# Low parts of weights by an accumulating DMA, and a fourth unit of weights ahead

## The chip, the cores and the metric

One core of a Trainium2 chip runs the whole program. The metric is the device time of one execution in microseconds (us). A change of less than 0.2% of it, about 4 us here, can't be told from no change.

## The reference, cut to what matters

Two layers of an encoder over 1024 tokens and 1024 channels, in float32. `w_in` projects the normalised input `h` into the inputs of four mixers (Fourier, convolution, dilated window attention, pooling) and four gate paths; the gated mixer outputs are projected, weighted and projected once more:

```python
h = rms_norm(x, norm_g)
z = h @ w_in                                   # 1024 x 4352
...
for n, y in enumerate(branch_outs):
    y_n = (y * gate_paths[:, :, n]) @ w_branch[n]          # 256 x 1024
    mg = jax.nn.sigmoid(h @ w_gate[n] + b_gate[n])         # 1024 x 1024
    merged = mg * y_n if merged is None else merged + mg * y_n
return x + merged @ w_out                                  # 1024 x 1024
```

## The kernel before

Every operand of TensorE (PE) is a pair: `hi`, the value rounded to fp32r, and `lo`, the rest of it. A product is three matmuls: hi by hi, hi by lo, and lo by hi (`passes`, L129). The pairs are made by `split` (L105, L106): ScalarE (ACT) copies the float32 source into `hi`, and VectorE (DVE) writes `lo` as the source minus `hi`.

Weights come in units of 128 x 1024 (512 KB), by `load_unit` (L108): SyncE (SP) issues the load into one of two raw buffers `wr` (L116), and `split` makes two tiles `w` of it. The tiles stand in a ring of 6 (tag "w"), so three units are held at a time; `weight_form` takes tiles of the same ring for the gates (`wf`). A raw buffer is free again when its last reader, DVE's subtraction, is done. `high_priority(offset=AHEAD)` lets a scheduler place these instructions some 100 instructions early in the queues; each engine then runs its own queue strictly in order.

A layer goes through these stages (times of layer 0):

- up to 500 us: the input units (`in_unit`: one unit by 2 halves of the tokens, 48 matmuls of 512 columns). Between the matmuls, `tick` lets in pieces of the attention (products `s`, exponentials `p`, transposes `pt`, products `pv`, evacuations `o`), of the convolution's 31 taps (`cv`, on DVE) and of the Fourier mixer. DVE also makes `pl`, the low part of the transposed probabilities.
- 500 to 590 us: `branch`, 8 units by 48 matmuls, whose results `y` go to DRAM on SP's queue.
- 590 to 909 us: `gates`. Results `y` are read back on GpSimd's queue (POOL, L993).
- 909 to 1000 us: `out_proj`. The merged parts `mt` are loaded by SP and split into `m` (by `merged`), beside 8 units of `w_out` for each half of the tokens, 24 matmuls a unit. The last layer cuts its second half into quarters and keeps some units.

Four of POOL's instructions are small memsets of `up` (L621, L622) for the next layer. The first input units of a layer, and those of `begin`, use `load_unit` as well.

Of the kernel before, what the change touches and what calls it, by code (L numbers as in the profile page):

```python
# [10 lines left out]
F32R = mybir.dt.float32r  # L11
AF = mybir.ActivationFunctionType
ALU = mybir.AluOpType

P = 128
S = 1024
H = 512
KC = 8
# [3 lines left out]
NEG = -8e30  # L22
SLOTW = 1040
SLOTP = 1088
AHEAD = 100
LAG = 4
LAGT = 2
# [6 lines left out]
KEPT = (None, None, None, "H", "H", "H", "H", "M")  # L34
# [12 lines left out]
class Net:  # L47
# [37 lines left out]
    def slot(self, name, dt=F32, w=S, tag="A"):  # L85
        shape, bufs = {"H": (S, NH), "M": (S, NM), "A": (SLOTP, NA)}[tag]
        return self.sp.tile([P, shape], dt, tag=tag, name=name, bufs=bufs)[:, :w]
# [17 lines left out]
        self.nc.scalar.activation(out=hi, in_=src, func=AF.Copy)  # L105
        self.nc.vector.tensor_tensor(out=lo, in0=src, in1=hi.bitcast(F32), op=ALU.subtract)  # L106

    def load_unit(self, src, kc=KC, n=P, tag=None, ahead=AHEAD):  # L108

        raw = self.raw()  # L110
        flat = raw.rearrange("p k n -> p (k n)")[:, :kc * n].rearrange("p (k n) -> p k n", n=n)
        place = (lambda: self.slot("w", F32R, tag=tag)) if tag else (
            lambda: self.wp.tile([P, KC, P], F32R, tag="w", name="w", bufs=6).rearrange("p k n -> p (k n)"))
        out = [place()[:, :kc * n].rearrange("p (k n) -> p k n", n=n) for _ in range(2)]
        with self.tc.high_priority(offset=ahead):
            self.nc.sync.dma_start(out=flat, in_=src)  # L116
            self.split(*out, flat)
        return out

    def raw(self):  # L120
# [137 lines left out]
    def begin(self, units):  # L258
# [59 lines left out]
        for u, evac in later[3:]:  # L318
            self.half_unit(w_in(u, ahead=AHEAD), 1, evac)

# [3 lines left out]
        evac(hf, ps)  # L324

    def in_unit(self, l, u, evac):
        w = self.load_unit(self.a["w_in"][l, u])
        for hf in range(2):
            self.half_unit(w, hf, evac)

# [503 lines left out]
    def conv_slot(self, dt=F32):  # L834
        return self.sp.tile([P, SLOTP], dt, tag="C", name="cv", bufs=1)[:, :2 * H + 2 * PAD]

# [92 lines left out]

    def branch(self, l, n, g):  # L930
        for u in range(2):
            wh, wl = self.load_unit(self.a["w_branch"][l, n, u])
            for dd in range(4):
                for hf in range(2):
                    ps = self.aux("py") if (dd + hf) % 2 else self.mm("py")
                    self.gemm(ps, [v[:, 2 * dd:2 * dd + 2] for v in (wh, wl)], g, hf)
                    y = self.t2("y")
                    self.nc.scalar.activation(out=y, in_=ps, func=AF.Copy)  # L938
                    self.nc.sync.dma_start(out=self.y[l][n, 4 * u + dd, :, hf * H:hf * H + H], in_=y)
# [27 lines left out]
            yield  # L967

    def weight_form(self, src):
        f = self.wp.tile([P, KC, P], F32R, tag="w", name="wf", bufs=6)  # L970
        self.split(f[:, 0:4], f[:, 4:8], src)
        return f[:, 0:4], f[:, 4:8]

# [5 lines left out]
    def weight_forms(self, l):  # L979
# [4 lines left out]
        for dp in range(4):  # L984
            for n in ORDER:
                raw = self.raw(), self.spare(flip)
                flip = 1 - flip
                ys = [self.slot(f"y{d}", tag="A") for d in range(2)]
                with self.tc.high_priority(offset=AHEAD):
                    for r, d in zip(raw, range(2)):  # L990
# [96 lines left out]
    def out_proj(self, l, tail):  # L1087
        nc = self.nc
        last = l == DEPTH - 1
        xin = self.a["xT"] if l == 0 else self.x1  # L1090
        if not last:
            self.h = self.new_h()
        ms = [[], []]
        self.start("m", self.merged(l, 0, "A", tail, ms[0]))
        self.finish("m")
        self.start("m", self.merged(l, 1, "H", tail, ms[1]))
        kept = {}
        Q = H // 2
        for o, n in ((0, H), (H, Q), (H + Q, Q)) if last else ((0, H), (H, H)):
            hf, off = o // H, o % H  # L1100
            sl = slice(o, o + n)
            xs = []
            self.finish("m") if hf else None
            m = [{hf: [x[:, off:off + n] for x in xk[hf]]} for xk in ms[hf]]
            acc = self.t2("acc")[:, :n]
            for d in range(KC):
                w = kept.get(d) if n < H else None
                if last and n == H and d >= 5:
                    kept[d - 2] = self.load_unit(self.a["w_out"][l, d - 2], tag="H")
                if w is None:  # L1110
                    w = self.load_unit(self.a["w_out"][l, d], tag=KEPT[d] if n < H else None)
                if n < H:
                    kept[d] = w
                ps = self.mm("op")[:, :n]
                self.gemm(ps, w, m, hf)
                if d % (S // n) == 0:
                    group = self.slot(f"xn{d}", tag="M").rearrange("p (d t) -> p d t", t=n)
                x = group[:, d % (S // n)]
                with self.tc.high_priority(offset=AHEAD):
                    nc.sync.dma_start(out=x, in_=xin[d, :, sl])  # L1120
                nc.vector.tensor_tensor(out=x, in0=ps, in1=x, op=ALU.add)
                if not last:
                    nc.sync.dma_start(out=self.x1[d, :, sl], in_=x)
                self.sq_acc(acc, x, d == 0)
                xs.append(x)
            if last:
                def emit(k, t, sl=sl):
                    nc.sync.dma_start(out=self.a["out"][k, :, sl], in_=t)
                self.start("norm", self.norm(acc, xs, lambda k: self.fg[:, k:k + 1], emit, f"f{o}"))
            else:  # L1130
                self.start("norm", self.norm(acc, xs, lambda k: self.p(l + 1, C_G + k), self.h_emit(self.h, hf), f"n{l}_{hf}"))
        if last:
            self.finish("norm")
# [138 lines left out]
```

## Time and profile before

| | us |
|---|---|
| median of 3 runs (lowest to highest) | 1987.56 (1986.22 to 1989.28) |
| the profiled execution: its own time | 1990.16 |
| its span, first to last instruction | 1988.4 |
| PE busy (share of the span) | 1948.0 (98%) |
| DVE busy | 1485.0 (75%) |
| ACT busy | 999.9 (50%) |
| POOL busy | 41.1 (2%) |

The profiled execution took 1.8 us around its span, and 2.6 us more than the median. Busy times are sums over the span. Matmuls overlap and their ends are modelled, so PE's 98% still holds short waits, and what counts is which wait of PE ends last in a stage. The granted TensorE clock was 0.998 of full speed over the span, that is, its upper level of 2.4 GHz nearly throughout.

### The profile page before, as it was taken

The page shows a single profiled execution, that of the slowest core. Times are in us where ns is not written, and L with a number is a line of the kernel's source. Part 1 is how long each engine was busy: PE and PEld are TensorE (multiplying, and loading weights), DVE is VectorE, ACT ScalarE, POOL GpSimd, SP SyncE. Part 2 cuts the span into 40 slices and gives each one's busy share as a digit, 9 for nine tenths or more (in the row PEclk, how much of TensorE's full clock was granted, in tenths as well). Part 3 has the DMA queues.
Part 4 walks back from the last instruction along what each step waited for, and adds up shares of the span by engine and source line. Part 5 has one row for each costly group of instructions (what it writes and reads, how often), then busy time and mean ns, then how long its engine had stood idle before and what let it go on. Part 6 is the DMA issues. An engine that isn't in the chain of part 4 may idle for free.

```text
span 1988.4 us, 26782 instructions
## 1 busy us (share of the span) xinstructions
PE 1948.0 (98%) x9484; PEld 1624.7 (82%) x9484; DVE 1485.0 (75%) x2740; ACT 999.9 (50%) x1917; POOL 41.1 (2%) x90
## 2 busy tenths in 40 slices
PE   8999999999999999999999999999999999999997
PEld 6788887888888888887888888888888888888887
DVE  7598878886577777776655888888564877787764
ACT  6336655568574344444431456656775644443441
POOL 0000000000000000000000000000000000000000
PEclk9999999999999999999999999999999999999999
DMA  6243344423774433427421534433248823424443
GB/s 237 78 149 117 102 131 120 128 67 107 247 276 167 156 106 108 157 76 259 163 81 45 159 117 126 133 106 106 87 139 295 287 85 127 136 99 146 170 148 107
DMA packets 129446, 281.08 MB, mean 141 GB/s; under 512 B 32928, under 2 KB 37920, under 8 KB 129312
## 3 DMA queue, kind: packets, MB, share of 16 engines
q1 hardware_dynamic: 118368, 239.52, 37.0%
q0 software_dynamic: 10944, 39.85, 6.0%
q8 instruction: 75, 1.23, 0.3%
q14 instruction: 59, 0.48, 0.1%
HBM read 186.84 MB, written 67.30 MB: 128 GB/s over the span
## 4 chain that ended last, share of the span: by engine, by line
PE 81%; DVE 9%; ACT 4%; DMA 4%; issue 2%; SPq 0%; DVEq 0%; ACTq 0%
PE z L129 24%; PE ga L129 13%; PE g L129 9%; PE gb L129 8%; PE op L129 8%; PE py L129 8%; PE z L256 3%; DVE cv L849 2%; PE pv L129 2%; PE s L466 2%; PE pt L492 1%; DVE w L106 1%; ACT w L105 1%; ACT o L523 1%; DMA mt<-m 1%
## 5 line engine op out<-in xcount | busy, mean ns | idle before, releaser
L129 PE MATMUL z<-h,w 128*128 128x512 f32 x3000 | 741.4, 396 | 2.5 <-DVE gp L610 1.4
L129 PEld LDWEIGHTS z<-h,w 128*128 128x128 f32 x3000 | 546.8, 188 | 109.1 <-DVE gp L610 1.8
L106 DVE TENSOR_TENSOR w<-wr,w 128x1024 fp32r<-128x1024 f32 (+1 forms) x135 | 158.7, 1178 | 106.8 <-ACT w L105 90.9
L105 ACT ACTIVATE w<-wr 128x1024 fp32r<-128x1024 f32 (+1 forms) x135 | 137.9, 1023 | 172.7 <-PE z L129 80.3
L129 PE MATMUL g<-h,wf 128*128 128x512 f32 x768 | 184.5, 389 | 0.0
L129 PE MATMUL ga<-t,wf 128*128 128x512 f32 x768 | 184.5, 389 | 0.0
L129 PE MATMUL gb<-t,wf 128*128 128x512 f32 x768 | 184.5, 389 | 0.0
L129 PE MATMUL op<-m,w 128*128 128x512 f32 (+1 forms) x960 | 179.8, 348 | 2.8 <-DVE m L106 2.7
L849 DVE SCALAR_TENSOR_TENSOR cv<-cv,params 128x512 f32<-128x512 f32 x240 | 179.1, 746 | 2.3
L129 PE MATMUL py<-g,w 128*128 128x512 f32 x768 | 178.4, 391 | 0.8 <-DVE gp L610 0.5
L129 PEld LDWEIGHTS op<-m,w 128*128 128x128 f32 x960 | 153.9, 189 | 27.1 <-DVE m L106 4.4
L129 PEld LDWEIGHTS py<-g,w 128*128 128x128 f32 x768 | 143.1, 188 | 31.7 <-ACT y L938 1.3
L129 PEld LDWEIGHTS ga<-t,wf 128*128 128x128 f32 x768 | 144.2, 188 | 29.9
L129 PEld LDWEIGHTS gb<-t,wf 128*128 128x128 f32 x768 | 144.2, 188 | 29.9
L129 PEld LDWEIGHTS g<-h,wf 128*128 128x128 f32 x768 | 144.2, 188 | 29.9
L105 ACT ACTIVATE wf<-wr 128x512 fp32r<-128x512 f32 x144 | 91.0, 632 | 117.6 <-issue 46.3
L106 DVE TENSOR_TENSOR wf<-wr,wf 128x512 fp32r<-128x512 f32 x144 | 98.8, 686 | 19.4 <-ACT wf L105 18.1
L480 ACT ACTIVATE p<-p,nm 128x256 f32<-128x256 f32 (+2 forms) x192 | 87.9, 459 | 42.7 <-DVE nm L477 42.4
L105 ACT ACTIVATE wf<-s 128x512 fp32r<-128x512 f32 x64 | 40.5, 632 | 105.2 <-PE gb L129 62.6
L129 PE MATMUL ga<-h,wf 128*128 128x512 f32 x384 | 92.2, 389 | 0.0
L523 ACT ACTIVATE o<-pv 64x128 f32<-64x128 f32 x192 | 67.5, 351 | 48.1 <-PE pv L129 46.2
L129 PEld LDWEIGHTS ga<-h,wf 128*128 128x128 f32 x384 | 72.1, 188 | 15.0
(244 smaller groups left out, 2683.0 us busy)
## 6 DMA issues: line engine op xcount, KB each, us to landing
wr<-in_w_in_dram SPq DMA_DIRECT2D x75, 512.0 KB, 3.8
y<-y SPq DMA_DIRECT2D x128, 256.0 KB, 4.1
y<-y POOLq DMA_DIRECT2D x64, 512.0 KB, 4.8
wr<-in_w_gate_dram SPq DMA_DIRECT2D x48, 512.0 KB, 4.4
wr<-in_w_out_dram SPq DMA_DIRECT2D x32, 512.0 KB, 3.6
rot<-rt SPq DMA_DIRECT2D x192, 64.0 KB, 2.0
cv<-in_w_gate_dram SPq DMA_DIRECT2D x16, 512.0 KB, 4.9
wr<-in_w_branch_dram SPq DMA_DIRECT2D x16, 512.0 KB, 4.7
```

The source lines that it names most:

```text
L105: self.nc.scalar.activation(out=hi, in_=src, func=AF.Copy)
L106: self.nc.vector.tensor_tensor(out=lo, in0=src, in1=hi.bitcast(F32), op=ALU.subtract)
L129: self.nc.tensor.matmul(ps, w, x, start=(first and i + u == 0), stop=(i == n - 1 and u == 2), skip_group_check=open_)
L256: self.nc.tensor.matmul(ps, a[:, k], b, start=(k + j == 0), stop=(k == KC - 1 and j == 2))
L466: mm(s[i][h], q[h + j][:, qs], k[h][:, a:a + n], start=(j == 0), stop=(j == 2))
L480: nc.scalar.activation(out=ph, in_=ph, func=AF.Exp, bias=nm[:, h:h + 1], accum_out=st[:, t, 2 + h:3 + h])
L492: nc.tensor.transpose(pt[:rows[ci], cs], p[:, off:off + rows[ci]], self.ident)
L523: nc.scalar.activation(out=dst, in_=src, func=AF.Copy)
L849: self.tc.keep_in_program_order(nc.vector.scalar_tensor_tensor(out=y, in0=u[:, j:j + H], scalar=tap(j), in1=y, op0=ALU.mult, op1=ALU.add))
```

## The change

`load_unit` gets a second way (`late=True`). ACT writes minus the high part into the `lo` tile, then the high part into the `hi` tile, both from the raw buffer; a DMA on POOL's queue then reads the same weights from DRAM a second time and adds them onto the `lo` tile. DVE takes no part. It is used for the input units that go through `in_unit`, for all units of `branch`, and for the units of `out_proj` with d > 0 (those that are kept ahead for the last quarters stay as they were): 96 units in all, 26 and 29 of `w_in`, 16 of `w_branch`, 14 and 11 of `w_out`. The ring of `w` tiles grows from 6 to 8, so four units are held; the space for descriptors of GpSimd's DMAs falls from 8192 to 2048 bytes.

```diff
+NWT = 8
...
-    def load_unit(self, src, kc=KC, n=P, tag=None, ahead=AHEAD):
+    def load_unit(self, src, kc=KC, n=P, tag=None, ahead=AHEAD, late=False):
...
-            lambda: self.wp.tile([P, KC, P], F32R, tag="w", name="w", bufs=6).rearrange("p k n -> p (k n)"))
+            lambda: self.wp.tile([P, KC, P], F32R, tag="w", name="w", bufs=NWT).rearrange("p k n -> p (k n)"))
...
             self.nc.sync.dma_start(out=flat, in_=src)
-            self.split(*out, flat)
+            if late:
+                self.nc.scalar.activation(out=out[1], in_=flat, func=AF.Copy, scale=-1.0)
+                self.nc.scalar.activation(out=out[0], in_=flat, func=AF.Copy)
+                self.nc.gpsimd.dma_start(out=out[1], in_=src, accum_op=ALU.add)
+            else:
+                self.split(*out, flat)
...
-        w = self.load_unit(self.a["w_in"][l, u])
+        w = self.load_unit(self.a["w_in"][l, u], late=True)
...
-            wh, wl = self.load_unit(self.a["w_branch"][l, n, u])
+            wh, wl = self.load_unit(self.a["w_branch"][l, n, u], late=True)
...
-        f = self.wp.tile([P, KC, P], F32R, tag="w", name="wf", bufs=6)
+        f = self.wp.tile([P, KC, P], F32R, tag="w", name="wf", bufs=NWT)
...
-                    w = self.load_unit(self.a["w_out"][l, d], tag=KEPT[d] if n < H else None)
+                    w = self.load_unit(self.a["w_out"][l, d], tag=KEPT[d] if n < H else None, late=d > 0)
...
-    nc = _bacc.Bacc("TRN2", target_bir_lowering=False, num_devices=1, dynamic_dma_scratch_size=8192)
+    nc = _bacc.Bacc("TRN2", target_bir_lowering=False, num_devices=1, dynamic_dma_scratch_size=2048)
```

The new lines move the numbers below them by one to six: L105 and L106 become L106 and L107, and the two new ACT copies are L119 (minus the high part) and L120 (the high part).

The order in which instructions stand shows what moves. First DVE in the attention of layer 0, at the piece of one head pair in which `qa` and `qb` are rotated and a `pl` is made. Before:

```order
L106 TENSOR_TENSOR w<-wr,w 128x1024
L382 TENSOR_TENSOR qa<-rot,qa 64x4x128
L382 TENSOR_TENSOR qb<-rot,qb 64x4x128
L849 SCALAR_TENSOR_TENSOR cv<-cv,params 128x512
L375 TENSOR_TENSOR rc<-rt,cos 128x512
L849 SCALAR_TENSOR_TENSOR cv<-cv,params 128x512
L106 TENSOR_TENSOR pl<-pt,ph 128x256
```

Now:

```order
L573 TENSOR_TENSOR xm<-xm,nat_2938 128x16
L388 TENSOR_TENSOR qa<-rot,qa 64x4x128
L388 TENSOR_TENSOR qb<-rot,qb 64x4x128
L855 SCALAR_TENSOR_TENSOR cv<-cv,params 128x512
L107 TENSOR_TENSOR pl<-pt,ph 128x256
```

The subtraction `w` ahead of these is gone, and `rc` and a tap `cv` now stand elsewhere. Next ACT at the end of layer 0's gates, where the first units of `out_proj` are split (`c`, `p` are gates, `m` the merged parts). Before:

```order
L1047 ACTIVATE p_8196<-g 128x512
L105 ACTIVATE wf<-wr_8072 128x512
L105 ACTIVATE w<-wr 128x1024
L1036 ACTIVATE c_8227<-g,params 128x512
L105 ACTIVATE w<-wr 128x1024
L105 ACTIVATE m_8293<-mt 128x512
```

Now:

```order
L106 ACTIVATE w<-wr 128x1024
L1042 ACTIVATE c_8103<-c_8103,params 128x512
L1053 ACTIVATE p_8230<-g 128x512
L119 ACTIVATE w<-wr 128x1024
L1042 ACTIVATE c_8261<-g,params 128x512
L120 ACTIVATE w<-wr 128x1024
L119 ACTIVATE w<-wr 128x1024
L120 ACTIVATE w<-wr 128x1024
L1042 ACTIVATE c_8277<-c_8277,params 128x512
L106 ACTIVATE m_8327<-mt 128x512
```

The first unit (d = 0, not late) stands earlier by the two tiles that the ring gained; the second and third (d = 1, 2) follow as pairs of copies ahead of the first `m`. Last SP at the same place. Before:

```order
L116 DMA wr<-in_w_out_dram 128x1024 x2
L1120 DMA xn_8381<-in_xT_dram 128x512 x2
L1120 DMA xn_8470<-in_xT_dram 128x512 x2
L1120 DMA xn_8545<-in_xT_dram 128x512 x2
L1120 DMA xn_8620<-in_xT_dram 128x512 x2
L116 DMA wr<-in_w_out_dram 128x1024
L1080 DMA mt<-m_78 128x512 x6
L116 DMA wr<-in_w_out_dram 128x1024
```

Now:

```order
L117 DMA wr<-in_w_out_dram 128x1024 x2
L1126 DMA xn_8415<-in_xT_dram 128x512 x2
L117 DMA wr<-in_w_out_dram 128x1024
L1126 DMA xn_8506<-in_xT_dram 128x512 x2
L1126 DMA xn_8583<-in_xT_dram 128x512 x2
L1126 DMA xn_8660<-in_xT_dram 128x512
L117 DMA wr<-in_w_out_dram 128x1024
L1086 DMA mt<-m_78 128x512 x9
L117 DMA wr<-in_w_out_dram 128x1024
```

The load just ahead of the `mt` loads was the third of `w_out` (d = 2) and is now the fourth (d = 3).

## Rows read from the trace of the kernel before

**Rows 1.** The page: busy time by engine, and the chain that ended last by engine.

```profile
PE 1948.0 (98%) x9484; PEld 1624.7 (82%) x9484; DVE 1485.0 (75%) x2740; ACT 999.9 (50%) x1917; POOL 41.1 (2%) x90
...
PE 81%; DVE 9%; ACT 4%; DMA 4%; issue 2%; SPq 0%; DVEq 0%; ACTq 0%
```

**Rows 2.** The page's groups (part 5): the weight split, xcount | busy us, mean ns | idle before.

```profile
L106 DVE TENSOR_TENSOR w<-wr,w 128x1024 fp32r<-128x1024 f32 (+1 forms) x135 | 158.7, 1178 | 106.8 <-ACT w L105 90.9
L105 ACT ACTIVATE w<-wr 128x1024 fp32r<-128x1024 f32 (+1 forms) x135 | 137.9, 1023 | 172.7 <-PE z L129 80.3
```

**Rows 3.** What PE waited for, whole span: us in total, times, longest.

```profile
PE pv L129 <- DVE pl L106: 2.6, 3, 0.9
...
PE fb L594 <- ACT o L523: 2.2, 2, 1.1
...
PE pt L492 <- DVE nm L477: 1.3, 1, 1.3
...
PE z L129 <- ACT rt L371: 1.1, 1, 1.1
PE pt L492 <- ACT o L523: 0.8, 2, 0.5
```

**Rows 4.** Timeline of PE at three waits: start us, us, what [idle before <- releaser].

```profile
283.87 0.30 PE L466 MATMUL s<-kb,qb 128*128 128x128 f32 x1 [0.62 <-DVE pl L106]
...
303.51 0.39 PE L129 MATMUL pv<-pl,vfh 128*128 128x256 f32 x1 [0.87 <-DVE pl L106]
...
515.17 1.17 PE L129 MATMUL py<-g,w 128*128 128x512 f32 x4 [0.53 <-DVE gp L610]
```

**Rows 5.** Timeline of DVE ahead of the second of these waits.

```profile
298.46 1.22 DVE L106 TENSOR_TENSOR w<-wr,w 128x1024 fp32r<-128x1024 f32 x1
...
303.04 0.42 DVE L106 TENSOR_TENSOR pl<-pt,ph 128x256 fp32r<-128x256 f32 x1
```

**Rows 6.** Chain that ended last, 895 to 925 us: start us, us, what.

```profile
895.55 2.73 PE g L129 x12
...
898.36 1.24 DVE w L106
...
899.62 0.33 SPq L116
...
900.52 7.14 DMA mt<-m
...
913.38 1.14 DVE w L106
...
915.16 0.61 DVE m L106
...
915.82 9.21 PE op L129 x39
```

**Rows 7.** Windows: busy us (instructions) of PE, PEld, DVE, ACT, POOL; PEclk; DMA share, GB/s.

```profile
100.00:500.00 400.00, 389.41 (x2062) 326.61 (x2061) 327.42 (x728) 233.93 (x544) 0.00 (x0) 1.00 0.39 114
...
480.00:600.00 120.00, 117.49 (x532) 95.38 (x531) 79.73 (x141) 75.81 (x132) 1.19 (x2) 1.00 0.74 257
900.00:910.00 10.00, 10.00 (x46) 8.29 (x45) 5.61 (x9) 3.92 (x6) 0.00 (x0) 1.00 1.02 360
940.00:950.00 10.00, 10.00 (x45) 8.27 (x45) 4.38 (x6) 2.28 (x4) 0.00 (x0) 1.00 0.47 160
```

**Rows 8.** The page: DMA issues, median us from issue to landing.

```profile
y<-y POOLq DMA_DIRECT2D x64, 512.0 KB, 4.8
...
m<-y POOLq DMA_DIRECT2D x12, 512.0 KB, 6.4
```

**Rows 9.** Chain that ended last, whole span: one stretch of back-to-back matmuls.

```profile
1013.74 78.91 PE z L129 x348
```

**Rows 10.** Timeline of ACT, a gate of the last product.

```profile
898.31 0.69 ACT L1036 ACTIVATE c<-g,params 128x512 f32<-128x512 f32 x1 [1.61 <-PE g L129]
```

**Rows 11.** Timeline of POOL: the second pair of memsets.

```profile
933.16 0.10 POOL L621 MEMSET up<- 128x8 f32 x1 [17.80 <-DVE m L106]
```

## The prediction

> **What bounds the kernel now.** I read the page's busy times and chain first: PE is busy 1948.0 us of 1988.4 and is 81% of the chain that ended last, DVE 9%, ACT 4% [rows 1]. So the most that any change of the other engines can return is PE's own waits, 40.4 us by these rows, part of them the start and the end. Next the groups of the weight split: a subtraction of DVE costs 1.18 us, a copy of ACT 1.02 us, 135 of each [rows 2]. Then the view of waits, for PE alone. The reader is to see that no row there says that PE waited for a weight tile `w`: PE waits for DVE's `pl` and `nm`, and for ACT's `o` and `rt`, one to three times each [rows 3]. So the change can't gain by bringing weights sooner, only by what leaving DVE and loading ACT does to those other waits. The timelines tell which wait had a weight subtraction in front of it. Before three waits of PE, of 0.62, 0.87 and 0.53 us [rows 4], DVE had worked without a pause from a subtraction to the releaser; for the second the rows show 1.22 us of `w` at 298.46 and the late `pl` at 303.04 [rows 5]. Last the chain at the start of layer 0's `out_proj`: a product of the gates ends, DVE subtracts the first unit, that frees a raw buffer for SP's next `w_out` load, behind that load stand the `mt` loads, 7.14 us to land, then the splits of `m` with another weight subtraction of 1.14 us among them, then PE [rows 6]. Layer 1 has the same chain.
>
> **The change, step by step.** DVE loses 96 subtractions, ACT gains 96 copies, POOL gains 96 DMAs. In layer 0's attention (100 to 500 us) about 26 of them fall: 26 x 1.18 = 31 us off DVE's 327 (9%), 26 x 1.02 = 27 us onto ACT's 234 (11%) [rows 2, 7].
>
> *Subtractions directly ahead of a wait.* The three waits above are each shorter than the 1.18 us taken from the run of work before them, so all go: 0.62 + 0.87 + 0.53 = **-2.0 us**. What may be late next there is ACT, whose copy precedes the `lo` part; the bound is nothing gained.
>
> *DVE's other waits in the attention.* `pl` keeps 2.6 - 0.9 = 1.7 us and `nm` 1.3 us [rows 3], with no weight subtraction in the run before. DVE has 9% less to do, but its taps `cv` fill the gaps. Between 0 and -3.0 us I take a third: **-1.0 us**.
>
> *ACT's waits.* PE waited 2.2 + 1.1 + 0.8 = 4.1 us for ACT's `o` and `rt` [rows 3]. One copy of 1.02 us more per unit stands in the same queue, and whatever is behind a copy that waits for a free tile waits too. Between 0 and twice as much (+4.1) I take a third: **+1.4 us**.
>
> *What the adding DMA costs.* The trace holds none. The nearest rows: a plain load of 512 KB on POOL's queue lands 4.8 us after its issue, a store 6.4 us [rows 8]. For the engines' time: 257 GB/s at a share of 0.74 [rows 7] makes 347 GB/s at a full share, so 512 KB copied once is 1.5 us of all 16 engines. The adding DMA reads the source, reads the tile and writes it: one pass, 1.5 us, from below, three passes, 4.5 us, from above. I take two, 3.0 us, since source and tile are both read. In `branch` a unit lasts 48 matmuls of 78.91 / 348 = 0.227 us [rows 9], 10.9 us: 0.74 + 3.0 / 10.9 = 1.02 of the engines. In `out_proj` a unit lasts 24 of these, 5.44 us: 0.47 [rows 7] + 3.0 / 5.44 = 1.02. The attention, at 0.39, has room. A share of 1.02 was reached in the trace, at 360 GB/s [rows 7]. So it just fits, and costs **0**.
>
> That an adding DMA has two reads is also what the Trainium skill says (Collectives: The Full Stack, "Why ReduceScatter is half of AllGather"): the addition itself is free, the second source read halves the rate. By it the price would be 3.0 us and the sum unchanged; no run here shows it yet.
>
> *Arrival of the low part.* With four units held, a tile is freed three units before its use: 3 x 5.44 = 16.3 us in `out_proj`, 32.7 us elsewhere. After that come a copy (1.02), then the adding DMA (6.4 if it lands like the slower row): 8.9 us to spare at the tightest place. **0**; a landing of 15 us would use it up.
>
> *The start of `out_proj`.* The subtraction at 913.38 leaves the chain: -1.14. But the order on SP now puts the fourth `w_out` load ahead of the `mt` loads. It needs the raw buffer of d = 1, and that is free only after both its copies. The first, into the `lo` tile, waits for the same product that ends at 898.28 (895.55 + 2.73) [rows 6]; then come 1.02, a gate of 0.69 [rows 10] and 1.02: 901.0, against 899.6 before. So the `mt` loads start 1.4 us later. Together +0.3 a layer, less a little for an addition of the gates that the order puts ahead of the first `m`: **0** for both layers, bounds -2.3 and +2.8.
>
> *POOL's queue.* Two pairs of memsets stand between layer 0's `w_out` additions, and wait for DVE. The second ran at 933.2 [rows 11]; the addition behind it is d = 6. PE reaches d = 6 five units after d = 0 ends: 39 matmuls from 915.82 [rows 6] less 35 of them give 916.7, plus 5 x 5.44 = 943.9. That is 10.7 us later, 4 us more than a landing. **0**.
>
> Sum: -2.0 - 1.0 + 1.4 = -1.6. The profiled execution took 1990.16 us (span 1988.4 and 1.8 around it): 1988.6. It lies 2.6 above the median, so the median becomes **1986.0 us**. About 0.2%, 4 us, can be told from no change.
>
> **Rivals.**
> *DVE's relief works fully.* The three waits, the other 3.0 us and the 2.3 us at both starts of `out_proj` go, and ACT, busy for about 60% of the attention, hides its copies: -7.3, 1980.3. For it: DVE was over 80% busy in the attention against ACT's 58% [rows 7]. Against it: ACT feeds most of these chains.
>
> *The `mt` loads are held up.* From 900 to 910 us the engines were already at 1.02 [rows 7]. The additions of d = 1 and d = 2 now fall there, 3.0 us each beside six `mt` loads of 256 KB. If one of them delays the first `mt` by its whole 3.0 us, PE waits 3.0 a layer: +6.0, 1992.0. It decides once the first `mt` takes about a microsecond more than 7.14. Against it: `m` beyond the first is limited by DVE, not by DMA.
>
> A page of the Trainium skill (DMA: Bandwidth & Descriptors, "Issuing engines are not separate DMA queues") would put POOL's DMAs on the same 16 engines as SP's, interleaved; that speaks for this rival, and no row of before shows the two together here.
>
> *The adding DMA takes three passes.* Then `out_proj` needs 0.47 + 4.5 / 5.44 = 1.30. Over layer 0's 16 units, 87 us, that is 26 us of backlog less 8.9 to spare: +17; over the 38 us of the last layer's seven late units before the quarters 11 - 9 = +2; `branch` at 1.15 builds 13 us, which its 25 to spare hide. 1986.0 + 19 = 2005. It decides above two passes.
>
> **How the numbers follow.** The forecast, within 4 us of before, gets 0.42; full relief 0.30; late `mt` loads 0.15; three passes 0.10; 0.03 for something else. The likeliest case's own range is 1983.6 to 1991.5. Both signs are possible, so the range runs from below full relief (less 2.3 for a start of `out_proj` that loses more than its subtraction), 1978, to between late `mt` loads and three passes, 1998; outside lie most of the three passes and some of the relief, less than 2 in 10. Faster by over 0.2%: 0.32; within: 0.42; slower: 0.26.
>
> **What would show it.** Of DVE: 96 groups of `w` less, and `pl` no longer among PE's longest waits. Of ACT: `o` and `rt` up. Of the adding DMAs: a landing below 10 us, and a DMA share near 1.0 in `branch`. At `out_proj`: the `mt` loads 1 to 2 us later. I am wrong if PE waits for `w` tiles from a DMA, if the adding DMA costs more than two passes, or if the new order of the queues makes waits that no row of before shows.

## The result and the profile after

The changed kernel takes 2075.11 us (median of 4 runs, 2073.4 to 2078.71) against 1988.42 for the kernel before (4 runs, 1986.22 to 1989.29): a ratio of 1.044, 95% interval 1.0427 to 1.0453. It is 87 us slower, and far above the range that was forecast (1978 to 1998).

The page of the changed kernel: PE's busy time and its neighbours, the software queue (packets, MB, share of 16 engines; all of POOL's transfers are in it), and the chain that ended last by engine.

```profile
PE 1976.2 (95%) x9484; PEld 1637.8 (79%) x9484; DVE 1362.4 (66%) x2644; ACT 1079.3 (52%) x2014; POOL 124.7 (6%) x186
...
q0 software_dynamic: 24768, 90.19, 20.0%
...
PE 68%; DMA 13%; ACT 8%; DVE 7%; issue 3%; SPq 1%; DVEq 0%; ACTq 0%
```

The software queue in the page of the kernel before:

```profile
q0 software_dynamic: 10944, 39.85, 6.0%
```

PE, DVE and ACT answer to [rows 1]. DVE's busy time fell by 122.6 us and ACT's rose by 79.4, as the change intends, yet PE's share of the chain fell from 81 to 68% and that of DMA rose from 4 to 13%. PE is busy 28.2 us longer with the same 9484 matmuls, and the span is 83.2 us longer, so some 55 us are new idle time of PE. The software queue gives the price of an addition: 20.0% of 2071.6 us less 6.0% of 1988.4 is 295 us of all 16 engines, 3.07 us for each of the 96.

Where the time went shows when the starts of the first matmuls of each stage are set against each other, read from PE's timeline in the two traces:

| stretch | before, us | after, us | longer by |
|---|---|---|---|
| start to the first `py` (input units, attention, layer 0) | 513.1 | 528.3 | 15.2 |
| to the first `g` (`branch`) | 91.2 | 103.6 | 12.4 |
| to the first `z` of layer 1 (`gates`, `out_proj`) | 395.6 | 400.0 | 4.4 |
| to the first `py` of layer 1 | 488.4 | 506.3 | 17.9 |
| to the first `g` of layer 1 | 89.5 | 101.7 | 12.2 |
| to the last unit of `out_proj` of layer 1 | 393.4 | 414.8 | 21.4 |

No stage pays for all: every stage with adding DMAs in it is longer. Between the `gates`' first and last matmuls, where there are none, the two traces keep step to 0.01 us.

What PE waited for in the changed kernel (us in total, times, longest), which answers to [rows 3]:

```profile
PE py L135 <- ACT y L944: 14.3, 11, 2.4
PE pt L498 <- ACT p L486: 11.1, 6, 3.2
PE pv L135 <- DVE pl L107: 11.0, 8, 4.8
PE v_f L181 <- DVE acc L217: 8.6, 2, 7.2
...
PE op L135 <- DMA w<-in_w_out_dram: 5.8, 3, 3.1
```

PE did not wait for `w` in the attention or in `branch`; it did for 5.8 us in the last layer. All other rows name ACT and DVE. But those are late themselves. What DVE waited for over the span, of its waits for a DMA, in the changed kernel and then in the kernel before:

```profile
DVE rot L382 <- DMA rot<-rt: 32.9, 15, 6.9
...
DVE og L601 <- DMA og<-od: 27.2, 6, 8.1
DVE cv L852 <- DMA cv<-cu: 19.7, 6, 4.5
...
DVE gt L923 <- DMA unpark<-att: 12.4, 3, 6.9
...
DVE xm L573 <- DMA nat<-sc: 10.3, 4, 6.5
```

```profile
DVE gt L917 <- DMA unpark<-att: 8.3, 3, 4.1
DVE rot L376 <- DMA rot<-rt: 7.7, 5, 2.5
...
DVE og L595 <- DMA og<-od: 5.6, 3, 4.3
...
DVE cv L846 <- DMA cv<-cu: 4.2, 4, 1.9
...
DVE xm L567 <- DMA nat<-sc: 2.7, 2, 2.1
```

With the groups that are left out, DVE waited 127.8 us for transfers in the changed kernel and 40.8 before. These are the kernel's own transfers through DRAM: `rot` (64 KB), `og`, `cv` and `unpark` (256 to 271 KB), and `nat` (16 KB), which reads back what `sc` (4 and 8 KB) wrote. The longest new wait of PE in the attention shows how such a transfer becomes a wait. The chain that ended last, from 296 to 312 us:

```profile
297.76 4.74 DMA sc<-st
...
302.55 4.95 DMA nat<-sc
...
307.52 0.18 DVE xm L573
...
309.87 0.34 DVE pl L107
...
310.26 0.80 PE pv L135 x2
```

Two transfers of a few KB, `sc` and `nat`, take 4.7 and 5.0 us one behind the other. At the same place of the kernel before, `sc` took as long (4.8 us), but `nat` 2.2; now an addition that POOL issued at 298.80 us and that took 8.1 us to land is under way beside it. DVE stands at `xm` until `nat` lands, and behind it in DVE's queue are `qa`, `qb`, a tap and the `pl` that PE needs. PE stood for 4.8 us. The kernel before has this wait too, far shorter: on DVE's timeline it lies just ahead of the row of 298.46 us in [rows 5].

```profile
297.51 0.17 DVE L567 TENSOR_TENSOR xm<-xm,nat 128x16 f32<-128x16 f32 x1 [0.54 <-DMA nat<-sc]
```

What followed in the changed kernel is in the windows (busy us and instructions of PE, PEld, DVE, ACT, POOL; granted clock; DMA share, GB/s):

```profile
100.00:500.00 400.00, 378.83 (x1984) 316.97 (x1984) 289.87 (x676) 248.82 (x555) 21.67 (x25) 0.98 0.56 143
307.00:310.00 3.00, 0.00 (x0) 0.00 (x0) 2.43 (x5) 0.00 (x0) 0.00 (x0) 0.73 0.55 188
311.00:314.50 3.50, 3.50 (x10) 2.73 (x9) 3.24 (x10) 2.52 (x7) 0.00 (x0) 0.50 0.18 45
500.00:600.00 100.00, 91.46 (x404) 73.66 (x403) 40.35 (x76) 58.84 (x94) 7.11 (x8) 0.97 0.85 257
940.00:950.00 10.00, 9.74 (x29) 7.11 (x29) 10.00 (x18) 8.77 (x15) 1.00 (x3) 0.67 1.04 330
```

In 307 to 310 us PE ran nothing, and from 311 to 314.5 us the granted clock is 0.50, the lower level (1.2 GHz), with PE busy throughout: this wait cost a second time behind itself. That is where part of PE's 28.2 us of extra busy time comes from: over the span the granted clock is 0.985, against 0.998 before. The rows of 100, 500 and 940 us answer to [rows 7]: in the attention the share rose from 0.39 to 0.56, about `branch` from 0.74 (480 to 600 us) to 0.85 (500 to 600 us), not to the forecast 1.02 (the stage itself became longer). In `out_proj` it is 1.04 at the start, and 0.95, 0.91 and 1.00 in the 30 us behind that, about the forecast 1.02.

In `branch` larger transfers do the same. PE's longest row above names ACT's `y`, which moves the results out. The longest two of these waits in layer 0 lead back to `unpark`: `y` stands in ACT's queue behind `g`, and `g` needs the load. The second of them (chain that ended last, from 586 us):

```profile
586.25 8.22 DMA unpark<-conv
594.49 0.64 ACT g L106
```

This load took 8.2 us, where its median was 4.3 before. ACT had stood idle for 6.5 us, and PE then waited 1.9 us for the `y` behind `g`.

Last `out_proj`. The chain at its start, which answers to [rows 6]:

```profile
926.57 0.96 ACT w L120
...
927.55 0.33 SPq L117
...
927.97 10.88 DMA mt<-m
```

The hand-over to SP came with the second copy of ACT (926.57), as forecast, but only 0.4 us later than before, counted from the end of the gates' product, and not 1.4: the first copy had run at 923.21 us, ahead of that end. The `mt` load then took 10.88 us against 7.14. Median landings of three transfers in the changed kernel (us, last column), and before:

```profile
wr<-in_w_out_dram SPq DMA_DIRECT2D x32, 512.0 KB, 6.6
...
rot<-rt SPq DMA_DIRECT2D x192, 64.0 KB, 3.1
...
mt<-m SPq DMA_DIRECT2D x24, 256.0 KB, 8.3
```

```profile
wr<-in_w_out_dram SPq DMA_DIRECT2D x32, 512.0 KB, 3.6
rot<-rt SPq DMA_DIRECT2D x192, 64.0 KB, 2.0
...
mt<-m SPq DMA_DIRECT2D x24, 256.0 KB, 5.9
```

And of the 96 additions (shortest, median, longest):

```profile
DMA to landing us min/median/max: 5.2/7.2/9.9
```

In the last layer the late loads of `w_out` make a chain of their own (chain that ended last, from 1960 us):

```profile
1960.65 8.91 DMA wr<-in_w_out_dram
...
1970.60 1.05 ACT w L120
...
1971.67 6.86 DMA wr<-in_w_out_dram
```

A load of 8.9 us, the two copies of ACT, and only then the next load into the freed buffer, 6.9 us. ACT ends the first copy, which starts an addition, one microsecond before it ends the second, which starts the next load; so each load runs beside an addition.

### The profile page after: what moved, and what is told of

It reads as the page before. It is cut to its first block, busy times and chain, and to the rows that moved or that the text cites. A ratio compares the mean times of both kernels' runs of the same rounds, so it can differ in the third digit from the quotient of the medians.

```text
span 2071.6 us, 26876 instructions
## 1 busy us (share of the span) xinstructions
PE 1976.2 (95%) x9484; PEld 1637.8 (79%) x9484; DVE 1362.4 (66%) x2644; ACT 1079.3 (52%) x2014; POOL 124.7 (6%) x186
## 4 chain that ended last, share of the span: by engine, by line
PE 68%; DMA 13%; ACT 8%; DVE 7%; issue 3%; SPq 1%; DVEq 0%; ACTq 0%
PE z L135 21%; PE ga L135 12%; PE g L135 8%; PE gb L135 8%; PE op L135 6%; PE py L135 4%; DMA rot<-rt 2%; PE pv L135 2%; DMA wr<-in_w_out_dram 2%; PE z L262 2%; PE pt L498 1%; DVE cv L855 1%; PE s L472 1%; DMA og<-od 1%; DMA mt<-m 1%
## 5 line engine op out<-in xcount | busy, mean ns | idle before, releaser
L135 PE MATMUL py<-g,w 128*128 128x512 f32 x768 | 186.2, 400 | 17.5 <-ACT y L944 14.3
L135 PE MATMUL op<-m,w 128*128 128x512 f32 (+1 forms) x960 | 189.6, 359 | 11.4 <-DMA w<-in_w_out_dram 5.8
L135 PEld LDWEIGHTS op<-m,w 128*128 128x128 f32 x960 | 160.2, 197 | 39.6 <-DMA w<-in_w_out_dram 7.2
L119 ACT ACTIVATE w<-wr 128x1024 fp32r<-128x1024 f32 x96 | 101.5, 1057 | 134.5 <-PE z L135 52.6
L106 ACT ACTIVATE wf<-wr 128x512 fp32r<-128x512 f32 x144 | 90.0, 625 | 42.2 <-PE gb L135 24.6
L121 POOL DMA_DIRECT2D w<-in_w_in_dram x55 | 47.8, 870 | 929.3 <-ACT w L119 906.9
L120 ACT ACTIVATE w<-wr 128x1024 fp32r<-128x1024 f32 x96 | 100.6, 1048 | 3.5 <-PE gb L135 3.3
L107 DVE TENSOR_TENSOR wf<-wr,wf 128x512 fp32r<-128x512 f32 x144 | 97.7, 683 | 0.2
L1042 ACT ACTIVATE c<-g,params 128x512 f32<-128x512 f32 x32 | 22.1, 690 | 143.3 <-PE g L135 138.8
L1019 DVE TENSOR_TENSOR c<-ga,p 128x512 f32<-128x512 f32 x64 | 44.0, 688 | 74.7 <-PE ga L135 72.2
```

Source lines behind the costliest of these rows:

```text
L119: self.nc.scalar.activation(out=out[1], in_=flat, func=AF.Copy, scale=-1.0)
L120: self.nc.scalar.activation(out=out[0], in_=flat, func=AF.Copy)
L121: self.nc.gpsimd.dma_start(out=out[1], in_=src, accum_op=ALU.add)
L135: self.nc.tensor.matmul(ps, w, x, start=(first and i + u == 0), stop=(i == n - 1 and u == 2), skip_group_check=open_)
L1019: add = lambda o, a, b: nc.vector.tensor_tensor(out=o, in0=a, in1=b, op=ALU.add)
L1042: nc.scalar.activation(out=c, in_=c if src is None else src, func=AF.Sigmoid, bias=self.p(l, C_BG + 8 * n + 2 * dp + d))
```

## The experiments

Theory A, from the traces: the additions take time of the DMA engines on which the chains through DRAM depend, and a transfer beside one lands later (`rot` by 1.1 us in the median). Theory B: the order of the queues does it, by the longer ring, the pairs of copies on ACT, and what stands behind them. The runs of one paragraph shared a chip and the runs of the kernel before.

**Ring, traffic and order apart.** `e1_ring8` keeps the ring of 8 and the small descriptor space, and splits all units as before:

```diff
-        w = self.load_unit(self.a["w_in"][l, u], late=True)
+        w = self.load_unit(self.a["w_in"][l, u], late=False)
```

(and so in `branch` and `out_proj`).

> The ring of 8 and the smaller descriptor space alone; all weight units are split by ACT and DVE as before. Theory A (traffic: the 96 adding DMAs share the DMA engines with the transfers that the chains of the attention, of branch and of out_proj wait for) expects 1983 to 1993 us, as before. Theory B (order: the longer ring moves loads and splits forward, and what stands behind them on ACT and SP is late) expects a good part of the loss of 87 us, above 2000.

`e2_thin` keeps all of the change but the bytes:

```diff
-                self.nc.gpsimd.dma_start(out=out[1], in_=src, accum_op=ALU.add)
+                self.nc.gpsimd.dma_start(out=out[1][:, 0, :16], in_=src[:, 0, :16], accum_op=ALU.add)
```

> The changed kernel with every instruction and its order, but the adding DMA covers 16 of 1024 columns (so the low part of the weights is wrong outside them). Theory A expects the loss to go with the bytes: 1980 to 1995 us, with rot landing in about 2.0 us and the branch loads in about 4.7 us as before. Theory B (order of the queues, pairs of copies on ACT) expects 2040 to 2075.

`e3_shadow` keeps the old kernel and adds only the bytes, onto two tiles in turn:

```diff
+                sh = self.shadow()
                 self.nc.scalar.activation(out=out[0], in_=flat, func=AF.Copy)
+                self.nc.scalar.activation(out=sh[:, 0, :16], in_=flat[:, 0, :16], func=AF.Copy)
+                self.nc.gpsimd.dma_start(out=sh, in_=src, accum_op=ALU.add)
                 self.nc.vector.tensor_tensor(out=out[1], in0=flat, in1=out[0].bitcast(F32), op=ALU.subtract)
```

> The kernel before (ring of 6, low parts by DVE) with 96 adding DMAs of the same sizes at the same places onto two tiles that nobody reads; ACT writes 16 columns of such a tile to release each. Theory A expects most of the loss, 2030 to 2075 us, though nothing of the program waits for these DMAs. Theory B expects 1986 to 1996.

`e4_poolsub` gives DVE's subtractions to GpSimd, with no DMA added:

```diff
-                self.nc.scalar.activation(out=out[1], in_=flat, func=AF.Copy, scale=-1.0)
                 self.nc.scalar.activation(out=out[0], in_=flat, func=AF.Copy)
-                self.nc.gpsimd.dma_start(out=out[1], in_=src, accum_op=ALU.add)
+                self.nc.gpsimd.tensor_tensor(out=out[1], in0=flat, in1=out[0].bitcast(F32), op=ALU.subtract)
```

> Ring of 8, and for the same 96 units the low part is a subtraction on GpSimd instead of DVE: the relief of DVE without a byte of traffic and without a second copy on ACT. If DVE's relief is worth what the first rival of the prediction says, 1978 to 1984 us; if it is worth little, 1985 to 1991; above 1995 if the subtraction on GpSimd is so slow (over some 10 us) that PE waits for w, or if it slows DVE beside it.

| run | median, us (runs) | ratio to before (1986.95), 95% interval |
|---|---|---|
| `e1_ring8` | 1984.67 (10) | 0.9988, 0.9979 to 0.9997 |
| `e2_thin` | 1986.23 (10) | 0.9995, 0.9986 to 1.0004 |
| `e3_shadow` | 2068.44 (4) | 1.0409, 1.0391 to 1.0426 |
| `e4_poolsub` | 2051.27 (4) | 1.0319, 1.0303 to 1.0334 |

Theory B falls. With every instruction and its order kept (each engine's queue is the same in the two traces) and all but 1/64 of the bytes gone, the time is that of before: DVE's waits for transfers fall from 127.8 to 62.5 us, and PE's for `pl` from 11.0 to 1.0. With the bytes alone, which nobody waits for, 81 of the 87 us are there, and in the same stages (15.2 us to the first `py`, 18.7 in the second attention, 9.5 and 9.0 in the two `branch`). `rot` lands in 2.0 us in `e2_thin` and in 3.1 in `e3_shadow`.

`e4_poolsub` missed all that was expected but the last clause. GpSimd's subtractions are faster than feared, and DVE pays (groups by line of that run, then DVE's taps in the changed kernel):

```profile
L120 POOL TENSOR_TENSOR w<-wr,w 128x1024 fp32r<-128x1024 f32 x96 | 238.8, 2489 | 1122.2 <-ACT w L119 1010.2 <-PE g L134 47.8 <-PE vtr L423 23.5
L854 DVE SCALAR_TENSOR_TENSOR cv<-cv,params 128x512 f32<-128x512 f32 x240 | 208.3, 868 | 2.8
```

```profile
L855 DVE SCALAR_TENSOR_TENSOR cv<-cv,params 128x512 f32<-128x512 f32 x240 | 179.3, 747 | 2.9
```

A subtraction on GpSimd took 2.49 us, and the same 240 taps of DVE took 868 ns each and not 747. DVE was busy 1487.6 us with 96 subtractions fewer, against 1362.4 in the changed kernel: it got back nothing. The Trainium skill (SBUF — State Buffer, "Who interferes with whom") has this: a VectorE instruction with two inputs in SBUF contends with a GpSimd instruction that reads SBUF. The trace agrees.

**Stage by stage, and the price without the addition.** `e5_in`, `e6_branch` and `e7_out` each leave `late` in one of the three places, with the ring of 8:

```diff
-            wh, wl = self.load_unit(self.a["w_branch"][l, n, u], late=True)
+            wh, wl = self.load_unit(self.a["w_branch"][l, n, u], late=False)
...
-                    w = self.load_unit(self.a["w_out"][l, d], tag=KEPT[d] if n < H else None, late=d > 0)
+                    w = self.load_unit(self.a["w_out"][l, d], tag=KEPT[d] if n < H else None, late=False)
```

(the first of them, `e5_in`). `e8_plain` leaves out `accum_op=ALU.add` and nothing else.

> Adding DMAs for the 55 input units only (ring of 8 throughout). If the traffic of each stage costs what the comparison of the two traces puts down to it, the attentions lose 17 us each: about 1984.7 (ring of 8 alone) + 35 = 2020, between 2012 and 2028. If the loss is not local to a stage (later stages inherit it or give it back), outside this.

> Adding DMAs for the 16 branch units only. By the same table 12 us a layer: 1984.7 + 24 = 2009, between 2003 and 2016. If branch was late only because the attention's mixers came late, 1985 to 1995.

> Adding DMAs for the 25 units of out_proj only. By the same table 4 and 21 us: 1984.7 + 26 = 2011, between 2003 and 2017. If the last layer lost its time to stages ahead of it, 1985 to 1995.

> The changed kernel with its 96 extra DMAs as plain copies, which do not add (the low part then holds the whole weight): the same bytes read from DRAM, the same packets, but by the software queue's rows 1.5 us of the 16 engines each and not 3.1. If the engines' time is what costs, less than half of the loss, 2000 to 2030 us; if the bytes of DRAM or the number of packets cost, 2055 to 2075.

| run | median, us (4 runs each) | ratio to before (1988.14), 95% interval | over `e1_ring8` |
|---|---|---|---|
| `e5_in` | 2022.92 | 1.0175, 1.0157 to 1.0193 | 38.3 |
| `e6_branch` | 2005.77 | 1.0088, 1.0073 to 1.0103 | 21.1 |
| `e7_out` | 2012.25 | 1.0116, 1.0100 to 1.0132 | 27.6 |
| `e8_plain` | 2026.38 | 1.0190, 1.0175 to 1.0205 | 41.7 |

All four came as theory A had them. The starts of the stages show best that the losses are local. Against before, `e5_in` is longer by 14.7 and 17.7 us in the two attentions, `e6_branch` by 11.4 and 10.1 in the two `branch`, and `e7_out` by 4.0 and 20.8 in the two stretches that hold `out_proj`; all other stretches of these three lie between -3.3 and +1.2 us. In the medians the three places add up to 87.0 us over the ring of 8 alone, and the change is 90.4 over it. The kernel before moved by 1.5 us between these groups of runs; set against the medians of their own runs of before, the three add up to 83 us and the change to 89, so some 6 us may be common to the stages.

The plain copies cost 46% of the whole loss. Their row of the software queue:

```profile
q0 software_dynamic: 24768, 90.19, 14.4%
```

By it (of 2022.9 us) each took 1.8 us of the engines, 58% of 3.07. So the same packets and the same bytes read from DRAM cost less when they take less of the engines' time.

**Wherever, or only beside chains?** `e9_gates` puts 96 shadow additions into the `gates` of the kernel before, behind three of the weight forms (`beside`: ACT copies 16 columns into a shadow tile, then the adding DMA):

```diff
+                f = self.weight_form(a11)
+                self.beside(a11, self.a["w_gate"][l, n, 2 * dp])
-                yield self.weight_form(a11), ys
+                yield f, ys
...
```

> The kernel before (ring of 6) with 96 adding DMAs of 512 KB, the same dose as the change, onto tiles that nobody reads, all of them in the gates (48 a layer), where the DMA engines were at 0.34 to 0.43 and PE never waited. If the engines' time costs wherever it falls, 0.92 us for each as in the shadow run, 2050 to 2075 us. If it costs only where a chain through DRAM has no slack, 1984 to 1994 us, with a share near 0.85 in the gates.

`e10_out_raw4` is `e7_out` with four raw buffers and the ring of 6, and `e11_raw4` the same without `late`:

```diff
-NWT = 8
+NWT = 6
...
-        return self.wp.tile([P, KC, P], F32, tag="wr", name="wr", bufs=2)
+        return self.wp.tile([P, KC, P], F32, tag="wr", name="wr", bufs=4)
```

> Adding DMAs for out_proj only, as before (2012 us), but with four raw buffers and a ring of 6. If the last layer's 15 to 20 us come from two raw buffers that each hold a load of 7 to 9 us and two copies (about 9 us for two units where PE asks for more), four raw buffers give most of it back: 1992 to 2000 us, the late mt loads of about 3 us a layer left. If the engines' time itself is short there, 2007 to 2015.

> Control to the run before it and a candidate: no adding DMA, ring of 6, four raw buffers. Loads earlier, splits as before: 1983 to 1990 us, as ring of 8 alone.

`e12_1k` cuts each adding DMA of the change into four:

```diff
-                self.nc.gpsimd.dma_start(out=out[1], in_=src, accum_op=ALU.add)
+                for j in range(0, kc, 2):
+                    self.nc.gpsimd.dma_start(out=out[1][:, j:j + 2], in_=src[:, j:j + 2], accum_op=ALU.add)
```

> The changed kernel with each adding DMA cut into four of 256 columns, so packets of 1 KB for 4 KB, the same bytes. If a small transfer like rot is late because each of its packets waits its turn behind one long adding packet, shorter packets give a good part back: 2025 to 2055 us and rot landing in 2.2 to 2.7. If the time of the engines in all is what counts, 2070 to 2100, more where short packets cost more.

| run | median, us (runs) | ratio to before (1987.37), 95% interval |
|---|---|---|
| `e9_gates` | 2096.91 (4) | 1.0551, 1.0535 to 1.0567 |
| `e10_out_raw4` | 2005.91 (4) | 1.0098, 1.0081 to 1.0115 |
| `e11_raw4` | 1988.00 (10) | 1.0006, 0.9996 to 1.0015 |
| `e12_1k` | 2058.15 (4) | 1.0354, 1.0336 to 1.0373 |

`e9_gates` is slower than either expectation, and settles nothing, for it made a wait of its own. What ACT waited for in it (us in total, times, longest):

```profile
ACT sh L137 <- DMA wr<-in_w_gate_dram: 153.7, 28, 6.9
ACT sh L137 <- DMA sh<-in_w_gate_dram: 92.2, 30, 6.4
```

ACT, which feeds the `gates`, stood 92 us for the two shadow tiles to come free and 154 us for raw loads, with the weight forms queued behind.

`e10_out_raw4` gives back 9.7 of the 27.6 us (17.9 over its control `e11_raw4`), less than expected. PE's waits in it:

```profile
PE op L135 <- DMA w<-in_w_out_dram: 6.6, 5, 2.7
PE v_f L181 <- DVE acc L217: 3.3, 2, 1.9
```

More raw buffers shorten the last layer's chain (the wait behind it was 7.2 us in the changed kernel), but PE still waits for `w`: load, copy and addition one behind the other, the last with a median landing of 8.6 us there. So the two raw buffers are about a third of this stage's loss. The late start of `out_proj` is not in what is left: in `e10_out_raw4` its first matmul follows the `gates` as closely as before, though the `mt` loads landed in 8.0 us in the median. That the rest is load, copy and addition in series is read from the rows, not shown by a run.

`e12_1k` is 17 us faster than the change, outside both expectations and not for the reason given: `rot` landed in 3.3 us and not in less than 3.1, and the additions took more of the engines (22.2% of 2056.5 us, 3.5 us each). So the engines' time alone does not set the loss. By the starts of the stages it gains in the first attention (6.5 us longer than before, not 15.2) and in the last `out_proj` (13.7, not 21.4), and loses in `branch`. Why stays open.

**Three more runs.** The gates again, in the kernel before, paced by GpSimd itself (`e13_gates_free` two a pair of `y`, `e15_gates_one` one):

```diff
                     for y, d in zip(ys, range(2)):
                         nc.gpsimd.dma_start(out=y, in_=self.y[l][n, 2 * dp + d])
+                    for y, d in zip(ys, range(2)):
+                        sh = self.shadow()
+                        nc.gpsimd.tensor_copy(out=sh[:, 0, :16], in_=y[:, :16])
+                        nc.gpsimd.dma_start(out=sh, in_=self.a["w_gate"][l, n, 2 * dp + d], accum_op=ALU.add)
```

> 64 adding DMAs of 512 KB onto tiles that nobody reads, two for each pair of results y that the gates read back; GpSimd itself copies 16 columns of a y to release each, so ACT's and DVE's queues stay as before, which the first run in the gates did not keep (ACT waited there for the tiles of the additions). If the engines' time costs 0.92 us for each wherever it falls, 1988 + 59 = 2047, between 2035 and 2060; if it costs only where a chain through DRAM has no slack, 1984 to 1994.

> The same with one adding DMA a pair, 32 in all, about as many in a microsecond as the change puts into the attention. By 0.92 us each 2017 (2010 to 2025); by slack alone 1984 to 1992.

`e14_in_raw4` is `e5_in` with the two lines of `e10_out_raw4`.

> Adding DMAs for the 55 input units only, with four raw buffers and a ring of 6. If the attention's loss comes from raw loads that land late and hold up ACT's queue, four raw buffers give it back, below 2008 us. If it comes from the small transfers on the chains of the attention (rot, sc, nat, cv, cy), which a raw buffer does not help, 2015 to 2030, as with two (2023).

| run | median, us (runs) | ratio to before (1987.68), 95% interval |
|---|---|---|
| `e13_gates_free` | 1988.51 (10) | 1.0003, 0.9993 to 1.0012 |
| `e15_gates_one` | 1987.75 (10) | 1.0001, 0.9992 to 1.0011 |
| `e14_in_raw4` | 2024.89 (4) | 1.0185, 1.0170 to 1.0200 |

The window of the `gates` of layer 0 in `e13_gates_free`, in `e15_gates_one`, in the kernel before, and in `e9_gates` (columns as above):

```profile
600.00:900.00 300.00, 300.00 (x1326) 248.47 (x1325) 231.05 (x356) 124.01 (x193) 57.38 (x96) 1.00 0.68 186
```

```profile
600.00:900.00 300.00, 300.00 (x1325) 248.42 (x1324) 232.41 (x357) 124.11 (x193) 38.40 (x66) 1.00 0.54 158
```

```profile
600.00:900.00 300.00, 300.00 (x1325) 248.48 (x1325) 231.04 (x356) 124.66 (x193) 19.05 (x36) 1.00 0.37 128
```

```profile
600.00:900.00 300.00, 269.71 (x1136) 217.32 (x1135) 195.18 (x305) 109.00 (x215) 53.13 (x74) 0.97 0.73 186
```

This is the clearest reading of the study. 32 additions a layer raise the share from 0.37 to 0.68, 2.8 us each by the software queue (15.0% of 1988.0 us), and PE is busy for all of the 300 us as before. The `gates`' own loads land later there too (`wr` in 5.3 us in the median, not 4.4), but no engine waits for them. In `e9_gates` the share is hardly higher, 0.73, and PE loses 30 of the 300 us, because an engine that feeds it waits there. `e15_gates_one` stands nearest to the attention: the gates go from 0.37 to 0.54 and lose nothing; the attention goes from 0.39 to 0.56, and 15 to 18 us are lost. So the share of the DMA engines says little of the cost; whether a chain in the stage waits for a transfer says it. In the kernel before, DVE and ACT waited 10.7 us for transfers from 100 to 500 us, and 0.5 us from 600 to 900.

Four raw buffers change nothing in the attention: `e14_in_raw4` takes 2024.89 us against 2022.92, 36.9 over its control `e11_raw4` where `e5_in` is 38.3 over `e1_ring8`. What DVE waited for from 100 to 500 us in `e14_in_raw4`:

```profile
DVE rot L382 <- DMA rot<-rt: 11.5, 5, 5.1
DVE xm L573 <- DMA nat<-sc: 10.1, 2, 5.9
DVE cv L852 <- DMA cv<-cu: 9.1, 3, 3.6
```

The waits for these transfers are as long as with two raw buffers (9.2, 7.9 and 6.7 us in `e5_in`), while ACT's waits for raw loads are gone; so late raw loads that hold up ACT are not what costs the attention its time.

## Why the prediction was wrong

- **The step that failed** is the cost of the adding DMA: "The attention, at 0.39, has room", and of `branch` and `out_proj` "it just fits, and costs 0". The price was right: two passes and 3.0 us were taken, 3.07 were measured, and the rival of three passes falls. The Trainium skill has it that the second read halves the rate (Collectives: The Full Stack, "Why ReduceScatter is half of AllGather"); 3.07 us for an addition against 1.8 for a plain copy, 1.7 times, comes near that. Instead of nothing, the same bytes cost 81 us when no engine waited for them (`e3_shadow`). What failed is the test that was put to the price: whether the engines have time left over a stage. A chain that goes through DRAM and back does not wait for the average; it waits for its own transfer, and that landed later beside the additions, while in the gates a higher share cost nothing. The rows for it were there: the chain before had 4% of DMA [rows 1], and `rot`, `og`, `unpark` and `nat` stood among DVE's waits, `nat` just ahead of the row that [rows 5] shows. They were not read, because PE was asked only whether it waits for `w`.
- **The `mt` loads** were the one place where contention was weighed, as a rival at +3.0 us a layer. It was right there: the first matmul of `out_proj` came 3.07 and 2.48 us later in the two layers, measured from the end of the `gates`. Traffic did it and not the new order: in `e2_thin` the first matmul follows as closely as before. The 1.4 us that the sum gave to the order came out at 0.4, as told above. The mistake was to look for late landings at no other chain.
- **Arrival of the low part.** The landings, 7.2 us in the median and up to 9.9, would have fitted: 6.4 was taken, with 8.9 us to spare at the tightest place. But the term took the raw load for done when the tile came free. In the last layer the load waits for a raw buffer, and its median rose from 3.6 to 6.6 us; with a copy of 1.06 and an addition's 7.6 that makes 15.3 of the 16.3 us that a tile is free ahead, and PE waited 5.8 us for `w`.
- **What wasn't traffic came out near, by luck in part.** 1986.0 us was forecast, and `e2_thin`, the change without its bytes, takes 1986.23. That is 0.7 us below its own runs of before, with an interval from 2.8 below to 0.8 above, so it bears out neither the sum's 1.6 nor any term. By the starts of the stages the terms were off: at the first `py` `e2_thin` is 6.5 us ahead of before, 4.0 of which the ring of 8 alone has (`e1_ring8`), for which the sum had no term; it gives 1.6 and 2.0 back in the two `branch` stages and 3.0 in the second attention.
- **DVE's full relief**, the likeliest rival at 0.30, is worth nothing that shows: in `e2_thin` DVE has some 120 us less work than before (and ACT some 80 more), and it is no faster than `e1_ring8`, which has none of it.
- **Of the signs to watch**, the landings below 10 us came about, and the DMA share near 1.0 did in `out_proj` (1.04) but not in `branch` (0.85); both had been named as signs that the additions fit. PE's waits for ACT's `o` and `rt` hardly moved. `pl` did not leave PE's list; it rose from 2.6 to 11.0 us, by the chain shown above.
- **POOL's memsets** cost nothing that the trace shows.

Shown by runs: the loss is the traffic of the additions (`e2_thin`, `e3_shadow`), it is smaller when the same bytes take less of the engines' time (`e8_plain`, though not in proportion, and `e12_1k` took more of it and lost less), it is local to three stages (`e5_in`, `e6_branch`, `e7_out`), and it is not there where no chain waits for a transfer (`e13_gates_free`, `e15_gates_one`). Read from the trace alone: which transfers carry it in the attention and in `branch`. Open: most of the loss of the last `out_proj`, and why shorter pieces cost less.

The fastest version of the study is the ring of 8 alone: 1984.67 us, a ratio of 0.9988 (0.9979 to 0.9997) to the kernel before. Its 2 us are less than the 4 that can be told from no change.

## What to carry to other kernels

Before DMA traffic is added to a kernel that is bound by an engine, read what the feeding engines wait for, and list every chain that goes through DRAM, however small its transfers: their landing times, not the share of the DMA engines, told here what the traffic cost. Where no chain waited for a transfer, traffic of the same kind was free in this kernel, so try to move it there. And test an added load by itself, as bytes that nobody reads: that run told the cause at once.

## What was not expected of the hardware

- A DMA share of 0.54 to 0.68 cost nothing in one stage, and one of 0.56 cost 15 to 18 us in another.
- A transfer of 16 KB (`nat`) took 4.95 us beside an addition, against 2.2 to 3.7 before; 64 KB (`rot`) landed in 3.1 us in the median against 2.0.
- An adding DMA of 512 KB from DRAM onto SBUF cost 3.07 us of the 16 engines (2.8 in the gates), the same DMA without the addition 1.8.
- Cut into pieces of 1 KB a partition, the additions cost the engines more (3.5 us) and the kernel less (2058 against 2075 us).
- A subtraction of 128 x 1024 on GpSimd took 2.49 us and slowed DVE beside it (its taps from 747 to 868 ns).
